# Where the feed-forward output rows are added up: in x2d with a copy afterwards, or in the output itself

## The chip, the cores and the metric

The kernel runs on one core of one Trainium2 chip. The metric is the device time of one execution in microseconds. The core has five engines: PE (TensorE, matrix products), DVE (VectorE), ACT (ScalarE), POOL (GpSimd) and SP (SyncE, which here only issues DMAs). Each takes its instructions strictly in the order in which they were written into its queue. The page counts the weight loads of PE as a line of their own, PEld.

## The reference, cut to what matters

One layer runs over a prompt of 2048 rows and over 128 sample rows (8 groups of 16), width 1024, everything in float32. After attention and the recurrent part, the layer ends with

```
x = x + rms_norm(mix, norm_g[1])                                  # this is x2
ffn, new_buf = conv_ffn(rms_norm(x, norm_g[2]), conv_buf, ...)    # up 1024 -> 2*2816, causal conv of 3 rows, gelu(gate)*up, down
x = x + rms_norm(ffn, norm_g[3])                                  # the output rows y
```

The change concerns the last line alone: how `x2 + rms_norm(ffn)` gets into the output.

## The kernel before

**Tiles and stages.** The rows form 17 tiles of 128 rows. The first half of the run (to about 1320 us) is attention and the recurrent part; it ends with x2 rows written to a DRAM buffer `x2d[t]`, one per tile. The rest is the feed-forward part, in three blocks of tiles (`FBLOCKS`: tiles 0-5, 6-11, and 12-15 with the sample tile). Each block has an *up stage*, a loop over 22 columns `f` of 128 hidden units, and a *down stage*. The three up stages lie about at 1320 to 1645, 1820 to 2140 and 2315 to 2605 us.

**One step f of an up stage.** SP loads weight quarters of 256 KB into `wu` buffers (L1339 in block 0, L1355 in the others; a ring of 11 buffers, `quad`). ACT rounds each to a high part (L1327) and DVE subtracts to get the low part (L1328). In block 0, DVE also forms four sums `ws` of them (L1344), which POOL stores to DRAM (L1346) for the later blocks. PE makes seven products into the PSUM tiles `ua`, `ub` and `uec`, each as three matmuls (L105 to L107). ACT and DVE add them up into rows `uu` and `ug`. POOL copies the two rows of halo for the convolution into and out of them (L1512, L1517; in block 2 also L1515 and L1516 for the sample rows). ACT and DVE convolve (`y`, L1520 on ACT, L1521 and L1522 on DVE, gelu at L1524 on ACT), and DVE multiplies gate and up (L1673; L1676 for the sample rows). POOL then issues the stores of `store_a` (L1594 to L1618) to the DRAM buffers `ad_A` and `ad_S`, from which the down stage reads. Two of these stores accumulate in DRAM; the one at L1618 waits for an earlier store to the same place to land.

**Rings that tie POOL to the others.** The rows `y` and `g` come from a ring of four (`row`). In block 2 each f takes three of them, so ACT can write `y` for step f+1 only when the stores that read `g` of step f-1 have landed. The rows `f`, `s` and `x` of 128x512 come from a ring of six (`spare_tile`).

**The delayed norm.** In blocks 0 and 1 the down stage does not finish its rows. `close` (L1745 to L1759) writes the two halves of the down product to `f0d[t]` and `f1d[t]`, makes the scale `rs`, and appends `(t, rs)` to `unfinished`. The next block's up stage finishes them in 12 units (6 tiles, two halves each), one for each f from `fi = 3` on: `done = delayed(...)`, driven by `next(done, None)` at L1623. A unit (`later`, L1440) has SP load the half row into `f` (L1445), DVE scale it (L1447, L1448), POOL issue a DMA that adds `f` onto `x2d` in DRAM (L1449), and POOL issue a copy of that half of `x2d` to the output (L1451), DRAM to DRAM. That copy waits on POOL until the accumulating DMA has landed. Block 2 finishes its own rows at the end and is not concerned.

**What sets the order.** A scheduler orders most instructions by a simulated timeline; what is wrapped in `tc.keep_in_program_order` keeps its place.

Of the kernel before, what the change touches and what calls it, by code (L numbers as in the profile page):

```python
# [13 lines left out]
ALU = mybir.AluOpType  # L14
# [36 lines left out]
def hymba_step(ctx: ExitStack, tc: tile.TileContext, I: dict, O: dict):  # L51
    nc = tc.nc
# [8 lines left out]
    def ps_mm(name):  # L61
        return psum.tile([P, 512], F32, tag="mm", name=name)

    def ps_big(name):
        return psum.tile([P, 1024], F32, tag="big", name=name)

    def ps_sm(name):
        return psum.tile([P, 512], F32, tag="sm", name=name)

    def spare_tile(name):  # L70
        return spare.tile([P, 512], F32, tag="k", name=name)

    def dt_(shape, name):
        return dram.tile(shape, F32, tag=name, name=name)
# [54 lines left out]
    x2d = [dt_([P, D], f"x2d{t}") for t in range(17)]  # L129
# [939 lines left out]
    def row(name):  # L1069
        return ffn.p3.tile([P, D], F32, tag="yq", name=name, bufs=4)  # L1070
# [348 lines left out]
    def out_rows(t):  # L1419
        return O["y_sample"] if t == SAMPLE else O["y_prompt"][t * P:(t + 1) * P, :]  # L1420
# [20 lines left out]
    def later(t, rs):  # L1441

        def unit(half):
            v, c = spare_tile(f"f{half}{t}"), slice(half * 512, half * 512 + 512)
            tc.keep_in_program_order(nc.sync.dma_start(v, (f0d, f1d)[half][t]))  # L1445
            yield 0.0, 0.0
            tc.keep_in_program_order(  # L1447
                nc.vector.scalar_tensor_tensor(v, v, rs, g3[:, c], op0=ALU.mult, op1=ALU.mult))  # L1448
            nc.gpsimd.dma_start(x2d[t][:, c], v, accum_op=ALU.add)  # L1449
            yield 0.0, 0.7  # L1450
            nc.gpsimd.dma_start(out_rows(t)[:, c], x2d[t][:, c])  # L1451
            yield 0.0, 0.0

        return [unit(half) for half in range(2)]

    def delayed(units):

        for u, old in zip(units + [iter([])], [iter([])] + units):
            next(u, None)
            yield  # L1460
            next(u, None)
            next(old, None)

    ph.close()
    p4 = ffn.p4 = ctx.enter_context(tc.tile_pool(name="p4", bufs=1, side="right", reuse_waits="tile"))
# [12 lines left out]
    def u_tile(name):  # L1478
        turns[0] += 1
        if turns[0] % 3:  # L1480
            return rows_tile("xr", [P, D], name)[:, :770]
        return p4.tile([P, 770], F32, tag="u", name=name)

    for b, tiles in enumerate(FBLOCKS):
# [8 lines left out]
        def product(i, w, acc, onto=False):  # L1493
            for k in range(4):
                c = slice(k * P, (k + 1) * P)
                mm3(acc[:, :n], w[0][:, c], w[1][:, c], B[i][:, 0, k, :n], B[i][:, 1, k, :n],
                    start=not onto and k == 0, stop=k == 3, onto=onto)

        def second(u, x, acc):

            add = lambda o, c, v=lambda t: t: nc.vector.tensor_tensor(o, v(x[:, c]), v(acc[:, c]), op=ALU.add)  # L1501
            if not last:
                add(u[:, 2 + n:2 + 2 * n], slice(0, n))
                return
            add(u[:, 2 + n + 64:2 + n + 192], slice(0, P))
            add(u[:, 2 + n:2 + n + 64], slice(2 * P, n))
            us = u[:, 2 + npr:2 + ln].rearrange("p (b s) -> p b s", b=DB)
            add(us[:, :, 2:DS + 2], slice(P, 2 * P), lambda t: t.rearrange("p (b s) -> p b s", b=DB))
# [18 lines left out]
        def ahead_of(i):  # L1527
            if i < 2 * NF:
                pend.append(load_up(b, i // 2, i % 2))
            elif i == 2 * NF:  # L1530
                pend.append(load_product(b, 0, 0) if fast else load_down(0, 0))
# [4 lines left out]
        def fetch(dh, k, early=False):  # L1536
            if dh > 1 or k >= NF:
                return
            if early:
                g[dh, k] = [quad(f"gr{b}_{dh}_{k}_{i}")[:, :n2] for i in range(2)]  # L1540
                for i, r in enumerate(g[dh, k]):
                    nc.sync.dma_start(r, gd[b][k][:, i * n2:(i + 1) * n2])
            else:
                g[dh, k] = row(f"gr{b}_{dh}_{k}")
                nc.sync.dma_start(g[dh, k][:, :2 * n2], gd[b][k][:, :2 * n2])
# [17 lines left out]
        def fetch_a(i):  # L1563
            if i >= 6 * len(SEQUENCE):
                return
            p, c = divmod(i, 6)
            src = ad[b, SEQUENCE[p][0]]
            ks = slice(2 * c, min(2 * c + 2, NK))
            n_ = (ks.stop - ks.start) * wide(p)
            if i < 5:  # L1570
                g[i] = [quad(f"ar{b}_{i}_{x}")[:, :384] for x in range(2)]
                for x, r in enumerate(g[i]):
                    nc.sync.dma_start(r, src[:, 2 * c + x, :])
            else:
                g[i] = row(f"ar{b}_{i}")[:, :n_]
                nc.sync.dma_start(g[i], src[:, ks, :].rearrange("p k n -> p (k n)"))

        def split_a(i):
            if i >= 6 * len(SEQUENCE):
                return  # L1580
            r = g.pop(i)
            n_ = 768 if isinstance(r, list) else r.shape[1]
            h_, l_ = w3_tile(f"ah{b}_{i}")[:, :n_], w3_tile(f"al{b}_{i}")[:, :n_]
            if isinstance(r, list):
                for x in range(2):
                    split(h_[:, x * 384:(x + 1) * 384], l_[:, x * 384:(x + 1) * 384], r[x])
            else:
                split(h_, l_, r)
            parts[i] = h_, l_
# [32 lines left out]
        for fi, f in enumerate(ORDERS[b]):  # L1622
            w = pend.pop(0)  # L1623
            ahead_of(2 * fi + 2)
            if fi >= 3:
                next(done, None)
            if fi == NF - 2:
                for i in range(2):
                    if fast:
                        fetch_a(i)  # L1630
                    else:
                        fetch(0, i, True)
            nm = f"{b}_{f}"
            a, d_, ec = ps_mm(f"ua{nm}"), ps_sm(f"ub{nm}"), ps_big(f"uec{nm}")
            e, c = ec[:, 0:512], ec[:, 512:1024]
            x1, x2, x3 = [p4.tile([P, 384], F32, tag="x", name=f"x{i}_{nm}", bufs=3) for i in range(3)]
            product(P1, w[0], a)
            nc.scalar.copy(x1[:, :n], a[:, :n])
            product(P6, w[1], d_)
            nc.vector.tensor_tensor(x2[:, :n], x1[:, :n], d_[:, :n], op=ALU.add)  # L1640
            product(P7, w[2], e)
            nc.vector.tensor_tensor(x3[:, :n], x2[:, :n], e[:, :n], op=ALU.add)
            product(P5, w[3], c)
            uu = u_tile(f"uu{nm}")
            second(uu, x3, c)
            w = pend.pop(0)
            ahead_of(2 * fi + 3)
            if fi == NF - 1:
                if fast:
                    split_a(0)  # L1650
                    split_a(1)
                    for i in range(2, 5):
                        fetch_a(i)
                else:
                    split_g(0, 0, w3_tile)
                    split_g(0, 1, w3_tile)
                    for k in range(2, 5):
                        fetch(0, k, True)
            ug = u_tile(f"ug{nm}")
            product(P2, w[0], a, onto=True)  # L1660
            nc.scalar.copy(ug[:, 2:2 + n], a[:, :n])
            product(P4, w[1], e, onto=True)
            nc.vector.tensor_tensor(uu[:, 2:2 + n], x2[:, :n], e[:, :n], op=ALU.add)
            product(P3, w[2], c, onto=True)
            second(ug, x2, c)
            yu = conv(uu, 1, f)
            yg = conv(ug, 0, f)
            gt = yg if fast and not last else row(f"g{nm}")
            gv, ov = (lambda t: t[:, :npr]), gt[:, :npr]
            if last:  # L1670
                gv = lambda t: t[:, :npr].rearrange("p (a n) -> p a n", a=2)
                ov = gt[:, :768].rearrange("p (a n) -> p a n", a=2)[:, :, 0:256]
            nc.vector.tensor_tensor(ov, gv(yg), gv(yu), op=ALU.mult)  # L1673
            if last:
                sv = lambda t: t[:, npr + 2:npr + 2 + DB * (DS + 2)].rearrange("p (b s) -> p b s", b=DB)[:, :, 0:DS]
                nc.vector.tensor_tensor(gt[:, 256:384].rearrange("p (b s) -> p b s", b=DB),  # L1676
                                        sv(yg), sv(yu), op=ALU.mult)
            if fast:
                store_a(f, gt)
            else:  # L1680
                nc.gpsimd.dma_start(gd[b][f][:, :nt * P], gt[:, :nt * P])
# [318 lines left out]
```

## Time and profile before

| what | value |
|---|---|
| three timed runs | 2757.23, 2759.12 and 2760.64 us (median 2759.12) |
| profiled execution, its own time | 2753.91 us |
| span from its first to its last instruction | 2752.2 us |
| mean granted clock of PE | 0.995 of full speed |
| DVE busy | 1922.8 us (70%) |
| ACT busy | 1457.1 us (53%) |
| POOL busy | 731.5 us (27%) |
| share of the DMA engines: queue q1 (SP's) / q0 (POOL's) | 47.2% / 14.8% |

The profiled execution took 1.7 us more than its span, and 5.2 us less than the median of the timed runs. In the views, a time is counted from the start of the span. The line of a "windows" view gives, for each engine, the busy time in that stretch and in brackets the number of its instructions, then the granted clock of PE, the mean busy share of the 16 DMA engines, and GB/s. In a "timeline", the bracket at the end of a row says how long the engine stood idle before that instruction and what ended it. In the "chain of waits", each row is a start, a duration, and who held the chain in that time.

### The profile page before, as it was taken

Reading aid. Unit: us, or ns where it says so; the run is one execution under the profiler, and the core shown is the slowest. Engines: PE = TensorE matmul, PEld = TensorE weight load, DVE = VectorE, ACT = ScalarE, POOL = GpSimd, SP = SyncE. Lnnn points to the kernel's source line nnn. Section 1 sums busy time; section 2 is a strip of 40 time slices with the busy share of each in tenths; the row PEclk is TensorE's granted clock in tenths of the full one; section 3 lists DMA queues with packets and bytes.
Section 4 is the critical chain, followed back from the end, with each engine's and each line's share of the span. In section 5 each row is a group of like instructions: output and inputs, shape, how many; then the busy total and the mean of one; then the engine's idle time right before and its main releaser. Section 6 shows DMA issues by size and latency. Waiting matters only on the chain.

```text
span 2752.2 us, 47852 instructions
## 1 busy us (share of the span) xinstructions
PE 2677.0 (97%) x16323; PEld 2504.0 (91%) x16323; DVE 1922.8 (70%) x3643; ACT 1457.1 (53%) x2961; POOL 731.5 (27%) x1397
## 2 busy tenths in 40 slices
PE   8999999999999999999999999999999999999998
PEld 7899999998899998878999997799999878999976
DVE  5344456646556667766999997758888866998956
ACT  4355545634356666543555456655455665554554
POOL 1000010211100002344465551123343212556401
PEclk9999999999999999999999999999999999999999
DMA  5534355557564456678776668757886867798875
GB/s 185 159 115 141 104 162 169 165 149 213 155 192 131 139 171 223 195 235 279 286 210 197 198 199 286 239 185 209 240 238 184 263 227 233 228 263 233 252 265 178
DMA packets 337172, 557.04 MB, mean 202 GB/s; under 512 B 62083, under 2 KB 168415, under 8 KB 336799
## 3 DMA queue, kind: packets, MB, share of 16 engines
q1 hardware_dynamic: 252846, 400.31, 47.2%
q0 software_dynamic: 45488, 119.84, 14.8%
q10 hardware_dynamic: 38592, 33.83, 3.7%
q8 instruction: 128, 2.10, 0.3%
q14 instruction: 118, 0.96, 0.1%
HBM read 389.77 MB, written 173.49 MB: 205 GB/s over the span
## 4 chain that ended last, share of the span: by engine, by line
PE 43%; DVE 4%; DMA 3%; issue 1%; ACT 1%; POOL 0%; SPq 0%; DVEq 0%; POOLq 0%; ACTq 0%
PE uec L105 5%; PE uec L106 5%; PE uec L107 5%; PE dn L107 3%; PE dn L105 3%; PE dn L106 3%; PE ua L107 3%; PE ua L106 3%; PE ua L105 3%; PE dnm L107 1%; PE dnm L106 1%; PE ub L107 1%; PE dnm L105 1%; PE ub L105 1%; PE ub L106 1%
## 5 line engine op out<-in xcount | busy, mean ns | idle before, releaser
L105 PE MATMUL uec<-B,wuh 128*128 128x384 f32 (+1 forms) x720 | 236.2, 328 | 6.0 <-DVE ug L1501 3.3
L106 PE MATMUL uec<-B,wuh 128*128 128x384 f32 (+1 forms) x720 | 235.3, 327 | 0.0
L107 PE MATMUL uec<-B,wul 128*128 128x384 f32 (+1 forms) x720 | 234.4, 327 | 0.0
L1327 ACT CAST wuh<-wu 128x512 fp32r<-128x512 f32 x255 | 141.7, 618 | 105.9 <-PE uec L106 104.5
L107 PE MATMUL dn<-wdh,al 128*128 128x512 f32 x462 | 186.0, 403 | 4.7 <-DVE al L1328 4.5
L1328 DVE TENSOR_TENSOR al<-ar,ah 128x768 fp32r<-128x768 f32 (+2 forms) x141 | 108.6, 779 | 116.4 <-ACT ah L1327 114.1
L105 PE MATMUL dn<-wdh,ah 128*128 128x512 f32 x462 | 183.8, 398 | 5.9 <-ACT ah L1327 3.7
L106 PE MATMUL dn<-wdl,ah 128*128 128x512 f32 x462 | 182.6, 395 | 0.0
L1327 ACT CAST ah<-ar 128x768 fp32r<-128x768 f32 (+2 forms) x141 | 96.2, 692 | 152.3 <-PE dnm L106 112.9
L1328 DVE TENSOR_TENSOR wul<-wu,wuh 128x512 fp32r<-128x512 f32 x255 | 164.5, 685 | 2.4 <-ACT wuh L1327 2.4
L406 DVE CUSTOM_DVE_ANT_0 tmp<-s,nb 128x640 f32<-128x640 f32 (+4 forms) x128 | 94.4, 738 | 89.9 <-PE s L396 89.3
L105 PE MATMUL vo<-wi_h,hT 128*128 128x256 f32 x544 | 155.2, 285 | 0.6 <-DVE mt L212 0.6
L107 PE MATMUL vo<-wi_h,hT 128*128 128x256 f32 x544 | 155.6, 286 | 0.0
L106 PE MATMUL vo<-wi_l,hT 128*128 128x256 f32 x544 | 154.8, 285 | 0.0
L1328 DVE TENSOR_TENSOR wdl<-wdr,wdh 128x512 fp32r<-128x512 f32 x231 | 145.5, 686 | 8.5 <-ACT wdh L1327 8.3
L105 PEld LDWEIGHTS uec<-B,wuh 128*128 128x128 f32 x720 | 135.2, 188 | 9.2 <-issue 3.7
L106 PEld LDWEIGHTS uec<-B,wuh 128*128 128x128 f32 x720 | 135.4, 188 | 0.2
L107 PEld LDWEIGHTS uec<-B,wul 128*128 128x128 f32 x720 | 135.1, 188 | 0.0
L105 PE MATMUL qk<-hT,wi_h 128*128 128x384 f32 (+1 forms) x384 | 129.0, 336 | 5.9 <-ACT qk_st L237 5.2
L419 DVE TENSOR_TENSOR ptl<-pt,pth 128x640 fp32r<-128x640 f32 (+4 forms) x128 | 93.6, 738 | 57.8 <-ACT pth L418 56.9
L1327 ACT CAST wdh<-wdr 128x512 fp32r<-128x512 f32 x231 | 127.5, 620 | 11.3 <-PE uec L106 7.5
L407 ACT ACTIVATE tmp<-tmp,mn 128x640 f32<-128x640 f32 (+4 forms) x128 | 97.6, 763 | 64.2 <-DVE mn L406 61.8
(426 smaller groups left out, 9258.8 us busy)
## 6 DMA issues: line engine op xcount, KB each, us to landing
wu<-in_w_up SPq DMA_DIRECT2D x220, 256.0 KB, 4.8
wu<-wsd SPq DMA_DIRECT2D x176, 256.0 KB, 3.4
wdr<-wtd SPq DMA_DIRECT2D x132, 256.0 KB, 4.8
wi_raw<-in_w_in SPq DMA_DIRECT2D x52, 512.0 KB, 4.0
wdr<-in_w_down SPq DMA_DIRECT2D x99, 256.0 KB, 4.7
wsd<-ws POOLq DMA_DIRECT2D x88, 256.0 KB, 4.3
ar<-ad_S SPq DMA_DIRECT2D x50, 384.0 KB, 3.4
kraw<-kTd SPq DMA_DIRECT2D x112, 128.0 KB, 3.3
```

The lines of the kernel that those rows point to most:

```text
L105: nc.tensor.matmul(out, ah, bh, start=start, stop=False, skip_group_check=onto)
L106: nc.tensor.matmul(out, ah, bl, start=False, stop=False, skip_group_check=onto)
L107: nc.tensor.matmul(out, al, bh, start=False, stop=stop, skip_group_check=onto)
L406: nc.vector.tensor_tensor_reduce(o_, s_, b_, 1.0, 3e38, ALU.add, ALU.min, accum_out=mn)
L407: nc.scalar.activation(tmp[:, :n], tmp[:, :n], AF.Exp, bias=mn, scale=-1.0, accum_out=rsum[:, i % 4, hh:hh + 1])
L419: nc.vector.tensor_tensor(s.ptl[:, sl, qc], ptv, s.pth[:, sl, qc], op=ALU.subtract)
L1327: nc.scalar.copy(h, r)
L1328: nc.vector.tensor_tensor(l, r, h, op=ALU.subtract)
```

## The change

The output rows of tiles 0 to 11 are first set to x2: in block 0's up stage, SP issues 12 copies of 512 KB from `x2d` to the output, DRAM to DRAM, one for each f from `fi = 3` to 14. The accumulating DMA of a unit then adds `f` onto the output rows themselves, and the 24 copies of 256 KB on POOL go away.

```
             tc.keep_in_program_order(
                 nc.vector.scalar_tensor_tensor(v, v, rs, g3[:, c], op0=ALU.mult, op1=ALU.mult))
-            nc.gpsimd.dma_start(x2d[t][:, c], v, accum_op=ALU.add)
+            nc.gpsimd.dma_start(out_rows(t)[:, c], v, accum_op=ALU.add)
             yield 0.0, 0.7
-            nc.gpsimd.dma_start(out_rows(t)[:, c], x2d[t][:, c])
-            yield 0.0, 0.0
...
     def delayed(units):
 
-        for u, old in zip(units + [iter([])], [iter([])] + units):
-            next(u, None)
+        for u in units:
+            next(u)
             yield
-            next(u, None)
-            next(old, None)
+            next(u)
...
             if fi >= 3:
                 next(done, None)
+            if b == 0 and 3 <= fi < 15:
+                tc.keep_in_program_order(nc.sync.dma_start(out_rows(fi - 3), x2d[fi - 3]))
```

The order on PE, DVE and ACT is the same in both kernels, instruction for instruction. POOL's differs by the copies and the destination alone. Here is POOL's queue in block 2's up stage before, at the unit that comes between steps 5 and 6: `uu_6` is the row that is convolved in step 6, `g_5` the row that step 5 stores, and `f` the scaled half row.

```order
L1449 DMA x2d_274<-f_28220 128x512
L1512 COPY uu_6_28618<-halo 128x2
L1451 DMA out_y_prompt<-x2d_274 128x512
L1515 COPY uu_6_28618<-sext 128x8x2
L1517 COPY halo<-ug_16_28462 128x2
L1516 COPY sext<-ug_16_28462 128x16
L1600 DMA ad_S_224<-g_5_28358 128x256
L1594 DMA ad_A_221<-g_5_28358 128x384
L1595 DMA ad_S_224<-g_5_28358 128x128
```

The same place of the changed kernel (its line numbers behind L1450 are 3 lower there):

```order
L1449 DMA out_y_prompt<-f_28214 128x512
L1509 COPY uu_6_28610<-halo 128x2
L1512 COPY uu_6_28610<-sext 128x8x2
L1514 COPY halo<-ug_16_28455 128x2
L1513 COPY sext<-ug_16_28455 128x16
L1597 DMA ad_S_224<-g_5_28352 128x256
L1591 DMA ad_A_221<-g_5_28352 128x384
L1592 DMA ad_S_224<-g_5_28352 128x128
```

The copy at L1451, with its wait, no longer stands between the accumulating DMA and the stores of `g_5`.

SP's queue in block 0's up stage, changed kernel, at one of the 12 places: `wu_0` to `wu_3` are the four quarters of one f, the row of L1625 is the new copy, and `wu_0_18290` begins the quarters of the next f.

```order
L1339 DMA wu_0_18125<-in_w_up 128x512
L1339 DMA wu_1_18127<-in_w_up 128x512
L1339 DMA wu_2_18129<-in_w_up 128x512
L1339 DMA wu_3_18131<-in_w_up 128x512
L1625 DMA out_y_prompt<-x2d_273 16x8192
L1339 DMA wu_0_18290<-in_w_up 128x512
```

Before, the two rows of L1339 around the copy stood directly behind each other. Nothing else moved on SP. The 12 copies stand behind the groups of four quarters number 5 to 16 (of 22).

## The prediction

> **What bounds the kernel now.** I read the page first, then the windows by stage, then the waits on the lines that change, and last the chain of waits where PE loses time. The page says that PE is the bound:
>
> ```profile
> span 2752.2 us, 47852 instructions
> PE 2677.0 (97%) x16323; PEld 2504.0 (91%) x16323; DVE 1922.8 (70%) x3643; ACT 1457.1 (53%) x2961; POOL 731.5 (27%) x1397
> ```
>
> So the change can only win where PE stands idle or slow. The windows of the three up stages (block 0, where the new copies go; blocks 1 and 2, where the old ones go away) show where that is:
>
> ```profile
> 1340.00:1640.00 300.00, 296.73 (x1685) 293.93 (x1684) 284.03 (x446) 152.67 (x244) 163.85 (x244) 0.99 0.66 201
> 1830.00:2140.00 310.00, 310.00 (x1781) 310.00 (x1780) 256.43 (x385) 154.47 (x253) 118.52 (x202) 1.00 0.75 212
> 2320.00:2590.00 270.00, 264.46 (x1771) 261.72 (x1770) 235.59 (x485) 144.84 (x256) 146.27 (x300) 0.99 0.80 232
> ```
>
> Block 1 has PE busy for 310 of 310 us: nothing can be won there. Block 2 loses time. Its 10 us slices say where: an undisturbed one holds 70 matmuls (first row), and these six hold fewer.
>
> ```profile
> 2390.00:2400.00 10.00, 10.00 (x70) 10.00 (x69) 8.86 (x19) 4.73 (x8) 3.68 (x8) 1.00 0.94 286
> 2400.00:2410.00 10.00, 9.51 (x65) 9.25 (x64) 10.00 (x20) 4.76 (x9) 8.36 (x14) 1.00 0.83 233
> 2440.00:2450.00 10.00, 8.98 (x62) 8.72 (x61) 9.51 (x22) 4.88 (x9) 7.45 (x15) 1.00 0.95 228
> 2480.00:2490.00 10.00, 7.76 (x50) 7.28 (x50) 6.02 (x15) 3.13 (x5) 4.89 (x11) 0.98 0.95 277
> 2490.00:2500.00 10.00, 9.59 (x47) 9.16 (x47) 7.63 (x15) 3.46 (x7) 6.67 (x17) 0.68 0.75 224
> 2520.00:2530.00 10.00, 9.55 (x66) 9.29 (x65) 7.59 (x17) 3.90 (x8) 8.78 (x19) 1.00 0.82 231
> 2530.00:2540.00 10.00, 9.07 (x57) 8.11 (x56) 9.26 (x20) 5.21 (x10) 4.55 (x11) 1.00 0.90 270
> ```
>
> They lack 5, 8, 20, 23, 4 and 13 matmuls, together 73 of 70 per 10 us, so 10.4 us. Two stalls carry most: 2480 to 2500 lacks 43 (6.1 us), and 2520 to 2540 lacks 17 (2.4 us). The first two slices (1.9 us together) I leave aside, since DVE is 9.5 to 10 of 10 us busy in them.
>
> Are the copies on POOL behind these two stalls? The view of L1451 says how long POOL stood before them, and how long a copy takes to land:
>
> ```profile
> L1451 POOL DMA_DIRECT2D out_y_prompt<-x2d x24: 541/566/573, 1902.0 to 2534.0; - x24
> ...
>   DMA x2d<-f: 59.2, 12
> ...
> DMA to landing us min/median/max: 3.1/4.3/7.3
> ```
>
> Twelve of the 24 waits alone hold POOL for 59.2 us, until its own accumulating DMA has landed. POOL's timeline ahead of the first stall:
>
> ```profile
> 2471.84 1.22 POOL L1449 DMA_DIRECT2D x2d<-f  x1
> 2472.40 1.40 POOL L1512 COPY uu<-halo 128x2 f32<-128x2 f32 x1
> 2478.64 0.57 POOL L1451 DMA_DIRECT2D out_y_prompt<-x2d  x1 [4.84 <-DMA x2d<-f]
> 2479.20 0.47 POOL L1515 COPY uu<-sext 128x16 f32<-128x16 f32 x1
> ...
> 2481.04 0.56 POOL L1600 DMA_DIRECT2D ad_S<-g  x1
> ...
> 2482.12 0.54 POOL L1595 DMA_DIRECT2D ad_S<-g  x1
> ```
>
> The three stores of `g` stand behind the wait. The chain of waits carries on from the last of them, and the timelines of ACT and DVE show what these two engines waited:
>
> ```profile
> 2482.12 5.39 DMA ad_S<-g
> ```
>
> ```profile
> 2487.62 0.93 ACT L1520 ACTIVATE y<-uu,wcv 128x656 f32<-128x656 f32 x1 [6.40 <-DMA ad_S<-g]
> ```
>
> ```profile
> 2488.58 0.90 DVE L1521 SCALAR_TENSOR_TENSOR y<-uu,wcv,y 128x656 f32<-128x656 f32 x1 [3.98 <-ACT y L1520]
> ```
>
> This is the ring of four rows: ACT's `y` needs the row that `g` holds until its stores land. DVE stands behind `y`, the low parts of the weights stand behind that on DVE, and PE waits for them. The second stall looks the same (POOL, ACT, DVE; the second row says when `g` was ready):
>
> ```profile
> 2510.95 0.89 POOL L1449 DMA_DIRECT2D x2d<-f  x1
> 2515.98 0.28 DVE L1676 TENSOR_TENSOR g<-y,y 128x128 f32<-128x128 f32 x1
> 2517.82 0.55 POOL L1451 DMA_DIRECT2D out_y_prompt<-x2d  x1 [5.98 <-DVE wu L1328]
> 2519.43 0.71 POOL L1517 COPY halo<-ug 128x2 f32<-128x2 f32 x1
> ...
> 2520.91 0.55 POOL L1606 DMA_DIRECT2D ad_S<-g  x1
> 2529.35 0.94 ACT L1520 ACTIVATE y<-uu,wcv 128x656 f32<-128x656 f32 x1 [6.10 <-DMA ad_S<-g]
> 2530.32 0.90 DVE L1521 SCALAR_TENSOR_TENSOR y<-uu,wcv,y 128x656 f32<-128x656 f32 x1 [2.73 <-ACT y L1520]
> ```
>
> **The change part by part.**
>
> *The copies leave POOL.* First stall: without the wait, `uu<-halo` ends at 2473.80. What then stands ahead of the first store took 2479.20 to 2481.04, 1.84 us, so that store goes out at 2475.6 instead of 2481.04, 5.4 us earlier. ACT's wait shrinks from 6.4 to 1.0 us, and DVE's of 3.98 goes, with 1.4 us to spare. Second stall: `g` is ready at 2516.26, and the halo copies that come between (2519.43 to 2520.91, 1.5 us) need rows of the same step, so the store goes out between 2516.3 and 2517.8 instead of 2520.91, 3.1 to 4.6 us earlier. ACT keeps 1.5 to 3.0 us of its 6.1, and DVE's 2.73 goes, with 0.4 us or more to spare. What is late next is PE itself. Both stalls together are 8.5 us. I take 8.0, since the spare is only 0.4 to 1.9 us and a later store may be met again. The bounds are 0 and the whole 10.4.
>
> The slow clock belongs to the first stall. PE's 5 us slices there:
>
> ```profile
> 2485.00:2490.00 5.00, 2.76 (x16) 2.28 (x16) 1.42 (x5) 2.38 (x4) 0.00 (x0) 0.96 1.02 306
> 2490.00:2495.00 5.00, 4.58 (x17) 4.17 (x17) 5.00 (x11) 2.71 (x6) 3.55 (x8) 0.50 0.46 109
> ```
>
> PE idles 2.24 us of the first slice, and in the second the granted clock is 0.50. Of the 6.1 us the second half (23 matmuls, 3.3 us) is this clock. I count it as gone with the idle time. The Trainium skill's "TensorE: Matmul & The Clock Gate" (Part 1) has the clock halved after an idle window of about 3.4 us; the trace's idle time is shorter, so by that rule alone the slow stretch might have another cause and stay. That is a rival below.
>
> *POOL's instructions in block 1, and the issues themselves* (24 of 0.57 us): nothing, PE is never short there.
>
> *SP's 12 copies of 512 KB in block 0.* They move the same bytes, from stages with 0.75 and 0.80 of the DMA engines busy into one with 0.66. PE does lose time in block 0, and it does so waiting for loads on the very queue that gets the copies. The timeline of SP, then of DVE, the slice of the stall, and all such waits from 1370 to 1530, where the copies go:
>
> ```profile
> 1473.05 0.33 SPq L1339 DMA_DIRECT2D wu<-in_w_up  x1
> ...
> 1486.14 0.33 SPq L1339 DMA_DIRECT2D wu<-in_w_up  x1
> ```
>
> ```profile
> 1480.21 0.69 DVE L1344 TENSOR_TENSOR ws<-wu,wu 128x512 f32<-128x512 f32 x1 [2.79 <-DMA wu<-in_w_up]
> ```
>
> ```profile
> 1480.00:1490.00 10.00, 8.54 (x48) 8.01 (x47) 9.79 (x16) 3.86 (x7) 5.69 (x8) 1.00 0.43 145
> ```
>
> ```profile
> DVE ws L1344 <- DMA wu<-in_w_up: 6.7, 4, 2.8
> ```
>
> The load issued at 1473.05 is `wu_3`, the last of its four, and DVE waits 2.79 us for it. A copy will be issued on the same queue right behind it. Four of these waits lie where the copies go; what a copy adds to them, PE loses. Bounds: nothing, if a queue serves in order (the copy is behind); or a whole landing of the copies that go away, 4.3 us, four times, 17.2 us. I take 0.2 us each, 0.8 in all, near the lower end, since the copy is issued last and the next group of loads follows only 13 us later (second row). SP's own issue (12 of about 0.33 us, the time of a row of these) lies in its wait for free buffers.
>
> *The accumulating DMA* keeps its size and place; its destination is the output. It gains a wait for the copy that SP issued in block 0, over 300 us earlier: nothing.
>
> The sum: 8.0 less 0.8, so 7.2 us. The profiled execution would go from 2753.9 to 2746.7. The timed runs lie 5.2 us above it at the median, and I carry the difference over: 2759.1 - 7.2 = **2751.9 us**.
>
> **The rivals.**
>
> *L1618 takes the wait over.* It also waits on POOL for a landing, and POOL will come to it sooner. In block 2 so far:
>
> ```profile
> POOL ad_S L1618 <- DMA ad_S<-g: 6.3, 4, 1.9
> ```
>
> A hold longer than the spare of 1.4 us brings the first stall back. For it: 1.9 us is longer than that. Against: the stores of the same step are ahead of L1618 and not held. If half of the 8.0 comes back, the sum is 3.2 us: 2755.9.
>
> *The copies delay `wu_3` (slower).* If copy and loads are served in turns, each of the four critical groups loses up to 4.3 us: 17.2 less 8.0, 9.2 us slower, 2768.3. It passes the bound of slower from (8.0 + 5.5) / 4 = 3.4 us per group. For it speaks that DVE has no slack there, against it the order on the queue. The Trainium skill's "DMA: Bandwidth & Descriptors" (Issuing engines are not separate DMA queues) says that transfers from all engines share the same 16 DMA engines and interleave: moved from POOL to SP, a copy costs them as much as before. The shares above agree that they are already busy.
>
> *The clock's slow stretch has its own cause*, and meets PE there or elsewhere. Then its 3.3 us stay, and the sum is 8.0 - 3.3 - 0.8 = 3.9: 2755.2. For it: 2.24 us idle is short. Against: the slice of 0.50 comes right behind the stall.
>
> *The change does not do what it says*: another wait keeps POOL as long, or the stores are late for other reasons, as in block 1, where the same waits cost PE nothing. Then the time stays at 2759.1.
>
> **How the numbers follow.** A measurement can tell about 0.2% from no change, 5.5 us here. Chances: forecast 0.62, L1618 0.20, clock 0.06, no effect 0.05, slower 0.07. The forecast is 1.7 us beyond the bound, so of its 0.62 I count 0.55 as faster; of L1618's, 0.04. That makes faster 0.59, slower 0.07, and 0.34 within. The range: at the low end the whole 10.4 won and 1.9 for the spread of the timed runs below their median, about 2747; at the high end no effect, with 0.4 us on top, 2759.5. It leaves out the slower rival and some scatter.
>
> **What would show it.** Right: no DMA wait of 5 to 7 us on POOL around L1449 in blocks 1 and 2; the slices of block 2 hold 69 to 71 matmuls but for one or two; no clock of 0.50 there; block 0's `ws` waits stay near 6.7 us and 2.8 at most. Wrong: ACT's L1520 still waits 5 us or more for `ad_S<-g` in block 2; L1618's waits grow past 3 us with PE idle behind them; or the `ws` waits grow by 3 us a group.

## The result, and the profile after

| | before | after |
|---|---|---|
| median of the timed runs | 2757.5 us (10 runs, 2748.6 to 2768.0) | 2748.4 us (10 runs, 2744.8 to 2754.8) |
| profiled execution, its own time | 2753.9 us | 2747.4 us |
| its span | 2752.2 us | 2745.7 us |

The ratio of after to before is 0.9967, with a 95% interval of 0.9956 to 0.9977. The change takes 9.1 us off (6.3 to 12.1 by the interval); 7.2 were predicted, 2751.9 us against 2748.4 measured. Of the 3.5 us between these two, 1.6 lie in the base (ten runs of before have a median of 2757.5, the three behind the prediction had 2759.1) and 1.9 in the change.

The page of the changed kernel begins with the same busy time on DVE, 23 us less on POOL and 4.7 us less on PE, which does the same 16323 matmuls:

```profile
span 2745.7 us, 47826 instructions
PE 2672.3 (97%) x16323; PEld 2500.7 (91%) x16323; DVE 1922.9 (70%) x3643; ACT 1456.3 (53%) x2961; POOL 708.5 (26%) x1373
```

The windows of the three up stages, after:

```profile
1340.00:1640.00 300.00, 295.70 (x1685) 292.36 (x1684) 284.87 (x443) 150.57 (x242) 160.94 (x244) 1.00 0.73 222
1830.00:2140.00 310.00, 310.00 (x1781) 310.00 (x1780) 256.17 (x386) 157.06 (x259) 103.54 (x191) 1.00 0.73 202
2320.00:2590.00 270.00, 268.61 (x1830) 267.77 (x1829) 242.17 (x499) 152.14 (x269) 148.19 (x297) 1.00 0.81 229
```

Blocks 0 and 1 hold as many matmuls as before (1685 and 1781). Block 2 holds 1830 in the place of 1771. At 70 per 10 us, 59 more are 8.4 us. Of the 10 us slices from 2390 to 2550, three still lack matmuls; the rows at 2480 and 2490 are where the first stall was:

```profile
2400.00:2410.00 10.00, 10.00 (x70) 10.00 (x69) 10.00 (x22) 6.43 (x12) 7.76 (x13) 1.00 0.75 205
2410.00:2420.00 10.00, 9.51 (x65) 9.24 (x64) 10.00 (x23) 5.21 (x9) 7.12 (x13) 1.00 0.93 276
...
2440.00:2450.00 10.00, 9.55 (x65) 9.28 (x65) 9.68 (x20) 5.00 (x9) 7.93 (x16) 1.00 0.94 200
...
2480.00:2490.00 10.00, 10.00 (x70) 10.00 (x69) 10.00 (x20) 6.17 (x12) 7.45 (x12) 1.00 0.86 217
2490.00:2500.00 10.00, 10.00 (x71) 10.00 (x70) 9.09 (x19) 3.64 (x7) 6.17 (x15) 1.00 1.03 299
...
2520.00:2530.00 10.00, 9.55 (x66) 9.29 (x65) 9.52 (x22) 5.21 (x9) 7.46 (x16) 1.00 0.88 241
```

They lack 5, 5 and 4, so 14 of 70 per 10 us, 2.0 us, where before lacked 73 (10.4 us). DVE is 9.5 to 10 of 10 us busy in all three. The clock is 1.00 in every one of these rows.

The length of block 2's up stage is what the experiments go by. It is read from the first matmul into `ua` and the last into `uec` between 2300 and 2620 us, in the view of these tiles (the two times in a row are the first and the last start). Before:

```profile
L105 PE MATMUL ua<-B,wuh x120: 305/308/468, 2314.7 to 2590.1; 128*128 128x320 f32 x120
...
L107 PE MATMUL uec<-B,wul x240: 304/308/312, 2319.8 to 2604.6; 128*128 128x320 f32 x120
```

After:

```profile
L105 PE MATMUL ua<-B,wuh x120: 305/308/312, 2317.7 to 2584.3; 128*128 128x320 f32 x120
...
L107 PE MATMUL uec<-B,wul x240: 304/308/312, 2322.7 to 2598.8; 128*128 128x320 f32 x120
```

So 289.9 us before and 281.1 after, 8.8 us less. (The longest matmul of `ua` is 468 ns before and 312 after: the half clock is gone.) The stage starts 3.0 us later in this profile, which is why the two spans differ by only 6.5 us. That is no loss to the copies in block 0: its up stage, ahead of the first of them, already starts 4.9 us later here (first matmul into `ub` at 1325.9, before 1321.0). The start moves between profiles of the same kernel too: a second profile of before, below, has block 2's at 2312.5.

How the stall went is seen at the place where the first one began. Before, the row `g` was ready at 2473.16 (2472.88 + 0.28), and its first store left at 2481.04, 7.9 us later:

```profile
2472.88 0.28 DVE L1676 TENSOR_TENSOR g<-y,y 128x128 f32<-128x128 f32 x1
```

After, in the timeline around the same step, the unit's accumulating DMA was issued at 2467.58, `g` was ready at 2475.59, and its store left at 2475.70:

```profile
2467.58 1.18 POOL L1449 DMA_DIRECT2D out_y_prompt<-f  x1
...
2475.31 0.28 DVE L1675 TENSOR_TENSOR g<-y,y 128x128 f32<-128x128 f32 x1
2475.70 0.57 POOL L1597 DMA_DIRECT2D ad_S<-g  x1 [0.25 <-DVE g L1675]
...
2485.47 0.94 ACT L1517 ACTIVATE y<-uu,wcv 128x656 f32<-128x656 f32 x1 [1.90 <-DVE uu L1662]
```

ACT's `y` (L1517 now) no longer waits for the store. It waits 1.90 us for its own input `uu`. These are PE's waits from 2320 to 2590, before:

```profile
PE ua L105 <- ACT wuh L1327: 2.4, 2, 2.2
PE uec L105 <- DVE uu L1663: 2.0, 3, 1.0
PE ua L107 <- DVE wul L1328: 1.2, 2, 0.8
```

and after, where the weights' high and low parts are never late:

```profile
PE uec L105 <- DVE uu L1662: 1.4, 3, 0.5
```

On POOL, the view of L1449 after shows what POOL waits for at an accumulating DMA now: in the main for DVE to make `f`, and for no DMA of its own.

```profile
L1449 POOL DMA_DIRECT2D out_y_prompt<-f x24: 841/888/1260, 1899.2 to 2518.2; - x24
...
  DVE f L1448: 10.8, 12
...
DMA to landing us min/median/max: 4.6/6.3/7.5
```

The other two things that the prediction watched, after: L1618 (L1615 now) in block 2, and the waits for loads in block 0 from 1370 to 1530.

```profile
POOL ad_S L1615 <- DMA ad_S<-g: 4.5, 3, 1.8
```

```profile
DVE ws L1344 <- DMA wu<-in_w_up: 6.5, 4, 2.6
ACT wuh L1327 <- DMA wu<-in_w_up: 1.9, 1, 1.9
```

Neither grew but for the one wait of 1.9 us on ACT, although a copy of 512 KB takes longer to land than the copies of 256 KB did (4.3 us at the median):

```profile
L1625 SPq DMA_DIRECT2D out_y_prompt<-x2d x12: 494/495/1164, 1362.9 to 1525.8; - x12
...
DMA to landing us min/median/max: 7.0/7.1/7.3
```

The Trainium skill's "DMA: Bandwidth & Descriptors" (Issuing engines are not separate DMA queues) has all issuers share the same 16 engines. The windows agree: the DMA share of block 0 rises from 0.66 to 0.73, and of block 1 falls from 0.75 to 0.73. The bytes have moved, and not gone. Block 2's share does not fall (0.80 before, 0.81 after): its window now holds 59 matmuls more, and so more of the stage's other transfers. Against a kernel as fast that keeps its copies in block 2 (0.85, below) it is lower.

### The profile page after: what moved, and what is told of

It reads as the page before. It is cut to its first block, busy times and chain, and to the rows that moved or that the text cites. A ratio compares the mean times of both kernels' runs of the same rounds, so it can differ in the third digit from the quotient of the medians.

```text
span 2745.7 us, 47826 instructions
## 1 busy us (share of the span) xinstructions
PE 2672.3 (97%) x16323; PEld 2500.7 (91%) x16323; DVE 1922.9 (70%) x3643; ACT 1456.3 (53%) x2961; POOL 708.5 (26%) x1373
## 4 chain that ended last, share of the span: by engine, by line
PE 42%; DVE 5%; DMA 3%; issue 1%; ACT 1%; POOL 0%; DVEq 0%; SPq 0%; POOLq 0%; ACTq 0%
PE uec L105 5%; PE uec L106 5%; PE uec L107 5%; PE dn L107 3%; PE dn L105 3%; PE dn L106 3%; PE ua L107 3%; PE ua L105 3%; PE ua L106 3%; PE ub L107 1%; PE ub L106 1%; PE ub L105 1%; PE dnm L107 1%; PE dnm L106 1%; PE dnm L105 1%
```

## The experiments

The theory: the gain comes from one thing, that the stores of `g` in block 2 no longer stand on POOL behind a copy that waits for the accumulating DMA. The first rival: it comes from the traffic that is gone from block 2. The second: the slow clock, or the whole stall, came by chance in the profile shown. And open is whether the copies on SP in block 0 cost something that hides part of the gain.

Each kernel ran in 5 rounds against before; ratios are to before on the same chip, and are not the quotients of the two medians beside them. Where it isn't said otherwise, the order of instructions on PE, DVE and ACT is that of before.

**The wait away, the copies kept.** All 24 copies stay on POOL, but stand two units later (some 25 us), when the data has landed. The accumulating DMAs keep their program order too, and so leave 5 to 16 us later in the stage than in the changed kernel:

```
-            nc.gpsimd.dma_start(x2d[t][:, c], v, accum_op=ALU.add)
+            tc.keep_in_program_order(nc.gpsimd.dma_start(x2d[t][:, c], v, accum_op=ALU.add))
...
-            nc.gpsimd.dma_start(out_rows(t)[:, c], x2d[t][:, c])
+            tc.keep_in_program_order(nc.gpsimd.dma_start(out_rows(t)[:, c], x2d[t][:, c]))
...
-        for u, old in zip(units + [iter([])], [iter([])] + units):
+        none = [iter([]), iter([])]
+        for u, old in zip(units + none, none + units):
             next(u, None)
             yield
-            next(u, None)
             next(old, None)
+            next(u, None)
```

> The kernel before with its 24 copies kept on POOL, but each issued two units (some 25 us) after its accumulating DMA, so that it finds that DMA landed. Bytes and DMAs are those of before. Theory (POOL's wait for the landing holds the stores of g, and the ring of y rows hands that to ACT, DVE and PE): 7 to 10 us faster than before, block 2's up stage with about 1815 to 1830 matmuls between 2320 and 2590 us, no POOL wait over 2 us at the copies. Rival (the gain is the traffic that block 2 no longer carries: 12 copies of 256 KB): within 2 us of before, about 1770 matmuls.

Measured: 2745.7 us against 2755.3, ratio 0.9972 (0.9963 to 0.9981). POOL waits for no accumulating DMA in block 2. The window of block 2:

```profile
2320.00:2590.00 270.00, 268.62 (x1823) 267.28 (x1823) 243.24 (x504) 150.53 (x264) 153.62 (x310) 1.00 0.85 242
```

The DMA share is above before's 0.80, and the matmuls are there all the same. The traffic rival falls.

**The wait kept, the copies away.** The changed kernel, with a DMA of 16 rows by 16 elements (1 KB) on POOL where the copy stood. It reads what the accumulating DMA has just written, and so waits for it:

```
             nc.gpsimd.dma_start(out_rows(t)[:, c], v, accum_op=ALU.add)
             yield 0.0, 0.7
+            nc.gpsimd.dma_start(probe[t][half], out_rows(t)[0:16, c][:, 0:16])
+            yield 0.0, 0.0
```

(`delayed` is that of before.)

> The changed kernel with the old wait put back without its traffic: where the copy stood, POOL issues a DMA of 1 KB that reads the rows just added up (into a spare DRAM buffer), and so waits for the accumulating DMA to land. The output is unchanged. Theory: most of the gain is lost again, within 3 us of before, ACT waits of 5 us or more for the stores of g are back in block 2. Rival (traffic): as fast as the changed kernel, 7 to 10 us under before.

Measured: 2755.1 us against 2755.3, ratio 1.0007 (0.9998 to 1.0015). The gain is gone. The windows of block 2 and of the first stall, and the waits from 2320 to 2590:

```profile
2320.00:2590.00 270.00, 265.30 (x1782) 263.33 (x1781) 236.25 (x485) 146.50 (x259) 145.45 (x302) 0.99 0.78 221
...
2490.00:2495.00 5.00, 4.30 (x15) 3.46 (x16) 5.00 (x13) 3.44 (x7) 1.58 (x5) 0.62 0.61 135
```

```profile
POOL probe L1453 <- DMA out_y_prompt<-f: 23.3, 6, 5.9
...
PE ua L105 <- ACT wuh L1327: 2.0, 1, 2.0
...
ACT y L1522 <- DMA ad_S<-g: 6.2, 1, 6.2
```

The timeline shows the same chain as before, from the accumulating DMA through the waiting read to the store of `g` and ACT's `y`:

```profile
2471.81 1.10 POOL L1451 DMA_DIRECT2D out_y_prompt<-f  x1
2478.95 0.53 POOL L1453 DMA_DIRECT2D probe<-out_y_prompt  x1 [5.85 <-DMA out_y_prompt<-f]
2482.48 0.57 POOL L1602 DMA_DIRECT2D ad_S<-g  x1
...
2488.77 0.93 ACT L1522 ACTIVATE y<-uu,wcv 128x656 f32<-128x656 f32 x1 [6.23 <-DMA ad_S<-g]
```

The reduced clock is back with the stall, at the same place: PE stands idle for 1.99 us, waiting for `wuh`, just ahead of it. In the window of block 2 every kernel with the wait has a mean clock of 0.99, and every kernel without it 1.00.

**Block 2 alone, and block 1 alone.** The change for tiles 6 to 11 (finished in block 2) or for tiles 0 to 5 (finished in block 1); the others go the old way:

```
+NEW = range(6, 12)      # or range(0, 6)
...
+            if t in NEW:
+                nc.gpsimd.dma_start(out_rows(t)[:, c], v, accum_op=ALU.add)
+                yield 0.0, 0.7
+                return
             nc.gpsimd.dma_start(x2d[t][:, c], v, accum_op=ALU.add)
...
+            if b == 0 and fi - 3 in NEW:
+                tc.keep_in_program_order(nc.sync.dma_start(out_rows(fi - 3), x2d[fi - 3]))
```

> The change for tiles 6 to 11 alone (the units in block 2's up stage); tiles 0 to 5 (block 1) are finished as before. Theory: all of the gain, 7 to 10 us under before, since PE has no idle time in block 1. Rival (traffic and waits count wherever they are): about half, 4 to 5 us.

> The change for tiles 0 to 5 alone (the units in block 1's up stage); tiles 6 to 11 are finished as before, so POOL's waits in block 2 are those of before. Theory: within 2 us of before, the stall near 2490 us is there. Rival (half of the gain): 4 to 5 us faster.

Measured: block 2 alone 2746.9 us against 2755.3, ratio 0.9969 (0.9959 to 0.9979): all of the gain. Block 1 alone 2757.9 against 2756.2, ratio 1.0014 (1.0001 to 1.0028): none, and rather a loss. The window of block 2, first of the kernel with the change there, then of the other:

```profile
2320.00:2590.00 270.00, 268.61 (x1826) 267.55 (x1826) 242.83 (x502) 151.48 (x266) 147.75 (x298) 1.00 0.81 230
```

```profile
2320.00:2590.00 270.00, 261.71 (x1747) 258.95 (x1746) 232.02 (x476) 145.51 (x255) 144.78 (x296) 0.99 0.80 230
```

**What the copies on SP cost.** In the first kernel the first half of the run writes x2 straight into the output rows, and no copy is left at all:

```
-    x2d = [dt_([P, D], f"x2d{t}") for t in range(17)]
+    x2d = [O["y_prompt"][t * P:(t + 1) * P, :] for t in range(12)] + [dt_([P, D], f"x2d{t}") for t in range(12, 17)]
...
-            if b == 0 and 3 <= fi < 15:
-                tc.keep_in_program_order(nc.sync.dma_start(out_rows(fi - 3), x2d[fi - 3]))
```

> The changed kernel without its 12 copies on SP: for tiles 0 to 11 the x2 rows are written straight into the output rows, and all readers of x2 read them there; the accumulating DMAs add to them as in the changed kernel. Theory (the copies in block 0 cost nothing, being behind the loads that DVE waits for): within 2 us of the changed kernel, so 7 to 10 us under before. Rival (the copies cost some tenths of a us in each of four groups, or push the stores of POOL): 1 to 3 us faster than the changed kernel.

Measured: 2746.1 us against 2755.3, ratio 0.9965 (0.9954 to 0.9976). That is the lowest ratio of all, but the interval holds the changed kernel's 0.9967. The windows of blocks 0 and 2:

```profile
1340.00:1640.00 300.00, 295.40 (x1680) 291.33 (x1679) 283.87 (x442) 149.48 (x240) 159.64 (x243) 1.00 0.66 202
...
2320.00:2590.00 270.00, 268.61 (x1830) 267.78 (x1829) 242.08 (x498) 152.19 (x269) 150.06 (x297) 1.00 0.81 230
```

Block 0 has its 0.66 of DMA share back, and no more matmuls than with the copies (1680 against 1685). Read from the first matmul into `ub` to the last into `uec`, block 0's up stage takes 338.5 us without copies and 338.1 with them: no loss can be seen.

The second kernel is the changed one with each copy issued ahead of the load of `wu_3` and not behind it. A few rows on PE, DVE and ACT in block 0 change places too.

```
             for i in range(4):
                 q.append(quad(f"wu{f}_{i}"))
+                if i == 3 and preset:
+                    t = preset.pop(0)
+                    tc.keep_in_program_order(nc.sync.dma_start(out_rows(t), x2d[t]))
                 nc.sync.dma_start(q[i], src(i))
...
+            if b == 0 and 3 <= fi < 15:
+                preset.append(fi - 3)
             ahead_of(2 * fi + 2)
...
-            if b == 0 and 3 <= fi < 15:
-                tc.keep_in_program_order(nc.sync.dma_start(out_rows(fi - 3), x2d[fi - 3]))
```

> The changed kernel with each of the 12 copies issued one load earlier, ahead of wu_3 instead of behind it; a few instructions of block 0 change places with their neighbours. Theory (the queue serves in order, so only what is ahead delays a load): wu_3 lands later by the time of a copy, some 1.5 to 3 us, in the four groups of which DVE waits for it, 6 to 12 us slower than the changed kernel. Rival (the place on the queue does not matter): within 2 us of the changed kernel.

Measured: 2748.8 us against 2756.2, ratio 0.9976 (0.9964 to 0.9988), so about 0.1% (2 to 3 us) worse than the changed kernel, which the intervals don't tell apart. The waits from 1370 to 1530:

```profile
DVE ws L1348 <- DMA wu<-in_w_up: 7.2, 4, 2.1
ACT wuh L1327 <- DMA out_y_prompt<-x2d: 2.8, 2, 1.6
```

The four critical waits are 0.7 us longer together, and ACT has two waits, 2.8 us in all, that are put down to a copy. That is within what the kernels scatter: these waits take 5.3 to 7.1 us in all in the kernels without copies of 512 KB (the one with the loads reordered aside), and up to 8.8 in one that has them behind the loads. The theory expected 6 to 12 us and missed: a copy ahead on the queue did not hold the load behind it for its own 7 us of landing. Between 1370 and 1530 us, the loads land after 6.0 us at the median and 7.3 at most, as far as landings are recorded (five or six of 44); in the changed kernel it is 5.2 and 6.8, and in the kernel without copies 5.5 and 7.2.

**The loads reordered.** The kernel without copies, with `wu_1` loaded last of the four in block 0, since the waits are for `wu_3` (the scheduler moves rows on PE and DVE in block 0 with it):

```
-            for i in range(4):
+            for i in (0, 2, 3, 1):
                 q.append(quad(f"wu{f}_{i}"))
-                nc.sync.dma_start(q[i], src(i))
-            a11, a12, a22, a21 = q
+                nc.sync.dma_start(q[-1], src(i))
+            a11, a22, a21, a12 = q
```

> The version that writes x2 straight into the output, with the four quarters of block 0 loaded in another order (0, 2, 3, 1): the first sum that DVE makes needs quarters 2 and 3, which now come one load earlier, and quarter 1 last. Theory (what PE still loses in block 0 is DVE's wait for the last quarter): 2 to 5 us faster than the version it starts from, so 10 to 14 us under before. Rival (the loads are late as a whole, since they wait for buffers): within 1 us of that version.

Measured: 2751.0 us against 2756.2, ratio 0.9983 (0.9970 to 0.9997), about 5 us worse than without the reordering. The window of block 0 holds 25 matmuls fewer than in that kernel, 3.6 us, and PE has a wait there that the others don't have:

```profile
1340.00:1640.00 300.00, 291.67 (x1655) 288.79 (x1654) 279.75 (x436) 146.62 (x234) 160.46 (x239) 0.99 0.65 199
```

```profile
PE uec L105 <- DVE x L1639: 7.9, 4, 4.7
```

A miss: PE now waits for DVE's row additions (`x`). That the other order of rows which came with the edit does this is likely, and was not tried by itself.

**The copies on SP alone.** Before, with the twelve SP copies added, into a buffer that nothing reads:

```
             if fi >= 3:
                 next(done, None)
+            if b == 0 and 3 <= fi < 15:
+                tc.keep_in_program_order(nc.sync.dma_start(spare_out[fi - 3], x2d[fi - 3]))
```

> The kernel before, plus the 12 new copies of 512 KB on SP in block 0, into a spare DRAM buffer that nobody reads; all else as before. Theory (a copy stands behind the loads that DVE waits for and costs nothing): within 2 us of before, the DVE waits for loads at the ws sums in block 0 about 6.5 us between 1370 and 1530. The prediction's own term: 0.8 us. Rival (copies and loads are served in turns): 5 to 17 us slower, those waits grow by 1.5 us or more a group.

Measured: 2762.7 us against 2756.2, ratio 1.0025 (1.0014 to 1.0036). That was not expected, and the profile does not put the loss where the copies are. The window of block 2, the waits of block 0, and ACT's wait in block 2:

```profile
2320.00:2590.00 270.00, 260.16 (x1737) 257.27 (x1736) 230.60 (x473) 145.08 (x255) 146.22 (x296) 0.99 0.80 228
```

```profile
DVE ws L1344 <- DMA wu<-in_w_up: 6.1, 5, 3.0
...
ACT y L1522 <- DMA ad_S<-g: 17.5, 4, 6.3
```

Block 0's waits are about those of before, and its up stage takes 340.2 us, inside the 335.3 to 341.4 of the kernels without such copies. Block 2 holds 34 matmuls fewer than before (4.9 us), and ACT waits for the stores of `g` four times. So the stalls that the change removes can be larger than in the profile shown. Four more runs asked whether that is chance, bytes, or the order of issues. The first is before itself, once more, without an edit.

> The kernel before, once more, as a yardstick for the others. Both theories: ratio within 0.15% of 1. Theory (the loss in block 2 sits in POOL's wait for its own accumulating transfer, and its size follows when that transfer lands): the profile shows at least one POOL wait of 5 us or more at the copies of block 2, a granted clock of 0.50 beside it, and 1760 to 1785 matmuls of 1 to 2 us between 2320 and 2590 us. Rival (the stall of the profile shown before was a chance event of one execution): no such wait, or at another place, and 1820 or more.

Measured: 2754.8 us against 2755.4, ratio 0.9997 (0.9986 to 1.0008). The two 5 us slices of the first stall:

```profile
2485.00:2490.00 5.00, 2.56 (x11) 1.63 (x10) 2.38 (x6) 3.35 (x6) 0.00 (x0) 0.88 0.87 256
2490.00:2495.00 5.00, 4.58 (x18) 4.49 (x18) 4.87 (x10) 1.75 (x4) 4.67 (x10) 0.50 0.59 163
```

The stall and its half clock are there again, at the same place of the stage (which starts 2.2 us sooner here): no chance event of one execution. Then before with 1-KB copies in the place of the 512-KB ones, twelve, sixteen and eight of them:

```
+                tc.keep_in_program_order(nc.sync.dma_start(spare_out[fi - 3][0:16, 0:16], x2d[fi - 3][0:16, 0:16]))
```

> The kernel before with twelve copies of 16 rows by 16 elements (1 KB) on SP at the places where the 512-KB copies of x2 stand, into a buffer that nothing reads: the same order of issues on SP, next to none of the bytes. The run with the full copies alone was 0.25% slower than before, and its profile lost the time in block 2, not where the copies are issued. If the order of issues did that (twelve more transfers on SP shift which later transfers of SP share a semaphore): 1.0015 to 1.0035, and longer POOL waits in block 2 than before. If the bytes did it: 0.999 to 1.001. If it was scatter of the stall from kernel to kernel: anything between, with block 2's stalls unlike both.

> The kernel before with sixteen 1-KB copies on SP in block 0 (twelve of them made it 0.15% slower, interval 0.02 to 0.28%, with next to no bytes; no engine but SP has another order). SP's transfers signal on eight semaphores in turn, so twelve more shift all later transfers of SP by four semaphores, and sixteen by none. Theory A (what costs is the shift, which lets stores and loads of block 2 wait for other transfers' semaphores): 0.999 to 1.001, and block 2's up stage 288 to 290 us as before. Theory B (what costs is the issue of more transfers on SP, or its delay of what follows): 1.0015 to 1.003. Theory C (the difference is chance or the point in time at which block 2 starts): anything within 0.3%, unlike the next run.

> The same with eight 1-KB copies: no shift of the semaphores either. Theory A: 0.999 to 1.001, as with sixteen. Theory B: about two thirds of what twelve cost, 1.001 to 1.0015. Theory C: unlike the run with sixteen.

Measured: twelve 1.0015 (1.0002 to 1.0028), sixteen 1.0014 (1.0004 to 1.0023), eight 1.0019 (1.0008 to 1.0030). The bytes are not needed for the loss. By the ratios alone the three can't be told apart, and the intervals leave both theories room. By the length of block 2's up stage, neither fits: with sixteen and eight, where the shift of semaphores (theory A) forecast no change from before (288 to 290 us), it takes 292.4 and 295.4, and the fewest transfers go with the longest stage, against a price per transfer (theory B). That is one profile each; chance from kernel to kernel (theory C) stays open. The window of block 2 with eight, and the view of the second accumulating DMA of that stage:

```profile
2320.00:2590.00 270.00, 259.99 (x1733) 256.28 (x1732) 232.74 (x479) 141.03 (x245) 144.48 (x289) 0.99 0.80 225
```

```profile
L1451 POOL DMA_DIRECT2D x2d<-f x1: 1180/1180/1180, 2386.3 to 2386.3; - x1
...
DMA to landing us min/median/max: 8.4/8.4/8.4
```

All kernels together, the stage read from the same rows as above, and this landing from the same view:

| kernel | POOL waits for its accumulating DMA in block 2 | ratio | up stage of block 2, us | landing of the second unit, us |
|---|---|---|---|---|
| before, shown / again | yes | 1 / 0.9997 | 289.9 / 290.2 | 6.6 / 6.9 |
| wait kept | yes | 1.0007 | 288.2 | 5.8 |
| copies alone | yes | 1.0025 | 294.8 | 8.3 |
| 12 / 16 / 8 small copies | yes | 1.0015 / 1.0014 / 1.0019 | 293.8 / 292.4 / 295.4 | 10.0 / 8.6 / 8.4 |
| block 1 alone | yes | 1.0014 | 292.9 | 10.2 |
| after | no | 0.9967 | 281.1 | 7.1 |
| late copies | no | 0.9972 | 281.2 | 5.4 |
| block 2 alone | no | 0.9969 | 281.1 | 7.1 |
| x2 in the output | no | 0.9965 | 281.1 | 8.2 |
| copy first / loads reordered | no | 0.9976 / 0.9983 | 281.1 / 281.1 | 6.8 / 7.3 |

Without the wait the stage takes 281.1 or 281.2 us in all six kernels, whatever else was edited. With it, the stage takes from 288.2 to 295.4, and it is longer (292.4 or more) in the five where the second unit lands after more than 8 us. In these five alone PE also has waits of 1.3 to 2.7 us in all for DVE's `uu` at a line (L1501 in before) that it does not wait for in the other kernels. That the late landing makes the stage longer is likely from this, and was not tried by itself. A landing of 8.2 us costs nothing where nobody waits for it on POOL. Why it lands later in these five is open: all of them add transfers on SP in block 0, over 800 us earlier, but the kernel with the wait kept has twelve such too, and lands in 5.8.

Block 1's up stage, from the first matmul into `ua` to the last into `uec`, takes 330.8 or 330.9 us in all fourteen profiles, with the wait and without it: there the wait costs PE nothing.

## Why the prediction held, point by point

- **The two stalls (8.0 us).** Right in place and mechanism, and in size as far as one profile tells. The slices from 2480 to 2500 are full now, and those from 2520 to 2540 lack 4 in the place of 17 (4 in the first, as before): 43 + 13 = 56 matmuls, 8.0 us. By the start and end of the stage it is 8.8 us. That the 8.0 come out to the tenth is in part luck: the prediction counted 8.5 and took 0.5 off in case a later store is met again. No store is met again; what a slice still lacks goes with PE's three waits of up to 0.5 us for `uu`, which every kernel without the wait has. The wait kept takes the gain away, the copies moved behind the landing bring it, and block 2 alone has all of it.
- **The first store 5.4 us earlier.** Too little: against the time at which `g` is ready, it leaves 7.8 us earlier (0.1 us behind `g` in the place of 7.9). The working had subtracted one wait from the queue as it stood; but the copies of earlier units had held POOL too (6.97 us at 2462.94), and without them the unit itself comes sooner, 8.0 us ahead of `g` in the place of 1.3. Where ACT was to keep 1.0 us of its wait for the store, it keeps none.
- **The 1.9 us of the two slices left aside.** Those at 2400 and 2440 lacked 5 and 8 before; after, with the stage 3.0 us later, those at 2410 and 2440 lack 5 and 5, with DVE 9.7 to 10 of 10 us busy. So 1.4 of the 1.9 us stayed, and leaving them aside was right.
- **The slow clock, counted as gone with the idle time.** Right for block 2. In its up stage a reduced clock is at the stall in both profiles of before and in the kernel with the wait kept, and no kernel without the wait has one there (all six have a mean of 1.00). The rival of a clock with its own cause falls. The price of 3.3 us was a little high: of the 23 matmuls put down to the clock, some 3 belong to the 0.41 us that PE stood idle in the same slice.
- **The SP copies (0.8 us).** Not told apart from nothing: 0.9967 with them and 0.9965 without, each good to about 0.1%. Block 0's up stage takes 338.1 to 340.2 us in the six profiles with such copies and 335.3 to 341.4 in the seven without (the one with the loads reordered aside), so a cost near the 0.8 of the sum is neither shown nor ruled out. The rival that they delay `wu_3` by over 3.4 us a group falls: the critical waits were 6.5 us in all with them, and 7.2 with the copy ahead of `wu_3`, against 6.7 before. So the prediction's reason for a low price, the place at the end of a group, does not carry it; with the copies ahead of `wu_3` the time was only 2 to 3 us longer, if at all.
- **L1618 as the next to hold POOL.** It did not: 4.5 us in 3 waits, before 6.3 in 4, and PE waits for nothing of it. Its longest wait, 1.8 us, is still above the 1.4 us that were to bring the first stall back, but ACT no longer waits for any store of `g` in block 2.
- **Block 1 and the issues: nothing.** Right. Block 1 holds 1781 matmuls in both and its up stage is 330.8 us long in both. The kernel with the change there alone was no faster.
- **The size of the whole.** 7.2 us predicted, 9.1 measured (6.3 to 12.1): inside the interval, and 1.9 too low at the median. By stages, block 2 gave 8.8 where 8.0 were counted, and the copies cost nothing that shows where 0.8 were. The sum took its price from one profile, whose time (2753.9) lay below the median of before (2757.5 over ten runs). The wait's cost in other kernels ran from 7 to 14 us of this stage (288.2 to 295.4 less 281.1), so one profile could give it only roughly.

## What to carry to other kernels

A DMA that must wait for the landing of the one ahead of it, on an engine that also issues stores, holds all of those stores for a landing time (here up to 7.0 us in block 2). Look for it not by that engine's busy share, but by whose buffers the held stores would free. Move the dependent transfer two units back, where its data has landed (here as good as taking it away), or let the accumulation write its last destination at once; and price it in the stage where PE is short, since the same wait cost nothing in block 1.

## What the runs showed of the hardware that was not expected

- PE's clock fell to 0.50 behind idle stretches of 2.24 us and 2.44 us (the 5 us slices at 2485 in the two profiles of before). The Trainium skill's "TensorE: Matmul & The Clock Gate" (Part 1) asks for an idle window of about 3.4 us; these runs show that less can be enough, so that a stall of 2 us cost about another 3. No threshold follows: in the profile of before, an idle stretch of 1.62 us that ends at 1573.9 is followed by a clock of 0.50 (1575 to 1578), and one of 1.98 us that ends at 1732.4 by 1.00 (1733 to 1736).
- Eight transfers of 1 KB on SP in block 0 came with a loss of 0.19% (0.08 to 0.30%), which lay over 800 us later: block 2's up stage is 5.5 us longer than before in that profile. Why is open. An edit in such a kernel can look costly at a place where it costs nothing; the stage table, not the whole time, told the two apart.
- A copy of 512 KB, DRAM to DRAM, landed in 7.0 to 7.3 us on SP (two of the twelve landings are recorded), next to the weight loads of 256 KB, whose critical waits were 6.5 us in all, before 6.7.
